# Keeping the residual stream in DRAM between the stages of a two-layer decoder, and eight more seven-product groups

## The chip, the cores and the metric

The kernel runs on one core of a Trainium2 chip. The metric is the device time of one execution in microseconds (us); a result is the median of several executions. The engines are named as in the profile: PE (TensorE, matrix products), DVE (VectorE), ACT (ScalarE), POOL (GpSimd), SP (SyncE, which here only issues transfers).

## The reference, cut to what matters

One sequence of 256 tokens of width 2048, in float32, goes through two layers:

```python
h = x
h = h + mamba2_mixer(rmsnorm(h, a_norm_w), a_in_proj, ..., a_out_proj)      # in-projection, scan, out-projection
h = h + (silu(g) * u) @ w_down[0]          # g, u = split(rmsnorm(h, f0) @ w_gate_up[0])
k, v, cum = shared_kv(h, kv_norm_w, w_kvf, b_f, k_norm_w)
h = h + forgetting_attention(rmsnorm(h, b_norm_w), k, v, cum, w_q, q_norm_w, w_o)
h = h + (silu(g) * u) @ w_down[1]          # g, u = split(rmsnorm(h, f1) @ w_gate_up[1])
```

Nearly all of the work is products of the 256 x K activations with large weights that are read once: in-projection (2048 x 10304), out-projection (4096 x 2048), gate/up (2048 x 11264, twice), down (5632 x 2048, twice), queries, keys and values (2048 x 2048 each), attention output (2048 x 2048).

## The kernel before

**Products.** A weight block is 512 rows by 512 columns; its K rows are four slices of 128. Each float32 weight is split into two parts, `hi` (ACT casts it, L272) and `lo` (DVE subtracts, L278), and each product of a slice with 128 tokens is three matmuls of 512 columns: activation hi by `whi`, activation hi by `wlo`, activation lo by `whi`. A *unit* is 512 KB of weights (two slices), loaded by SP into one of six buffers `wraw` (`RAW = 6`), split into one of four pairs of buffers `whi`/`wlo` (`SPL = 4`); a *piece* is what one split feeds, 12 matmuls. `stream` walks the pieces in a fixed order; it issues the splits four pieces ahead of the matmuls, and a load as soon as the splits that free its buffer have been issued. Work on results (adding to the residual, transposes, gating) is woven in by `flow`, a small planner with its own estimates.

**Pairs and groups.** `pair` multiplies the same activations with two column blocks, left and right. For a K block (`kg`) that is not listed in `crossed`, that is 4 units and 48 matmuls. For one that is listed, a `Group` computes the 2 x 2 block product (two token halves by two column blocks) with seven products in place of eight: 7 pieces in the order f, d, c, a, e, g, b, of 6 matmuls each, 42 in all. A group needs five loads: three plain units and two sums of weights (`c`, `a`), which are made in DRAM ahead of time: `next_sum` has SP copy one block to a `wsum` tensor and POOL add another to it by an accumulating transfer. When it is called is set by `PACE`, pairs of (end, n): up to load number `end`, one call every n loads. DVE forms two more sums within a group (L428). The activations of a listed block need their own sums, `xS` (a slot of the pool `slots`), made in `to_slot` where the block is written, or later by `add_sums`, half a block at a time: four sums on DVE, a cast on ACT, a subtraction on DVE.

**Which blocks are listed.** `WOUT` for the out-projection, `DN0` and `DN1` for the down projections, `(2,)` for the attention output, and in `ffn_up` `(1, 2)` for the gate/up pairs 1 to 9 and `(2,)` for the first and the last. If the last two listed numbers are neighbours, `pair` puts the second group behind the next plain left block.

**Residual.** `h` (256 x 2048, 16 KB of each partition) is a constant tile, loaded from `x` at load number 24 (`load_h`). At the end of each pair of the out, down and attention-output stages, `parts_to_h` and `done` add the results to it; `take` then transposes it into the slots of the next stage. There are 15 slots of 8 KB.

**Order of the stages.** In-projection with the scan (called "in" below), out-projection ("out"), gate/up ("gu0"), down ("dn0"), queries/keys/values with attention ("qkv"), attention output ("wo"), gate/up ("gu1"), down ("dn1").

Of the kernel before, what the change touches and what calls it, by code (L numbers as in the profile page):

```python
# [35 lines left out]

WOUT, DN0, DN1 = (4, 6), (3, 7), (3, 5, 7, 9)

# [3 lines left out]

PACE = ((24, 0), (224, 6), (440, 9), (760, 7), (2000, 9))

# [137 lines left out]
class Unit:  # L182


    def __init__(self, blk, kg, src, width, ks, step=2):
        self.blk, self.kg, self.src, self.width, self.ks = blk, kg, src, width, ks
        self.pieces = [list(range(a, min(a + step, len(ks)))) for a in range(0, len(ks), step)]
        self.raw, self.dead = None, False

# [42 lines left out]
def kernel(ctx: ExitStack, tc: tile.TileContext, xT_d, x_d, cols_d, rows_d, wdt_d, win_d,  # L232
# [4 lines left out]
    const = ctx.enter_context(tc.tile_pool(name="const", bufs=1))  # L237
    slots = ctx.enter_context(tc.tile_pool(name="slots", bufs=15))
    wraw = ctx.enter_context(tc.tile_pool(name="wraw", bufs=RAW))
# [67 lines left out]

    h = const.tile([P, NT, DM], F32, name="h")

# [26 lines left out]

    def pair(xs, sources, done, fills, crossed, parts):


        both = [Block(xs, d, f) for d, f in zip(done, fills)]  # L340
        x = Cross(*both, parts)
        order, rights = [], []
        adjacent = len(crossed) > 1 and crossed[-1] == crossed[-2] + 1
        for kg in range(len(xs)):
            us = [halves(b, kg, src[kg], ([0, 2], [1, 3])) for b, src in zip(both, sources)]
            if kg in crossed:
                if not (adjacent and kg == crossed[-1]):
                    order += rights
                    rights = []
                (b11, b21), (b12, b22) = us  # L350
                c, a = Sum(b22.src, b12.src), Sum(b22.src, b21.src)
                sums.extend((c, a))
                first = {"f": b12, "d": b21, "c": Unit(None, kg, c, NB, [1, 3]),
                         "a": Unit(None, kg, a, NB, [1, 3]), "g": b11}
                order.append(Group(x, first, xs[kg], kg == crossed[0], kg == crossed[-1]))
            else:
                for b, u in zip(both, us):
                    b.units += u
                order += us[0]
                rights += us[1]  # L360
        if adjacent:
# [120 lines left out]
    def stream(pre_load, pre_split):  # L482
# [12 lines left out]
        def load_on():  # L495
            while dead[0] < len(units) and units[dead[0]].dead:
                dead[0] += 1
            while loaded[0] < min(dead[0] + RAW, len(units)):
# [143 lines left out]
    def h_slot(dst, j, wcol):  # L642
        yield from to_slot(dst, lambda t, f: h[:, t, (4 * j + f) * P:(4 * j + f + 1) * P],
                           None if wcol is None else wcol + 4 * j)
# [25 lines left out]
    def of_h(j):  # L670
        return [[h[:, t, i * NB:(i + 1) * NB] for t in range(NT)] for i in (j, j + 1)]

# [21 lines left out]
    def out_stage(xs, w_d, wcol, crossed, summed=()):  # L694
# [5 lines left out]
        def done(j):  # L700
            def run(ps):
                for t in range(NT):
                    hb = h[:, t, j * NB:(j + 1) * NB]
                    yield tt(hb, hb, ps[t])
# [4 lines left out]
        def take(j):  # L709
            yield SYNC  # L710
            yield from h_slot(nxt[j], j, wcol)
            for t in range(NT):
                sumsq(h[:, t, j * NB:(j + 1) * NB], ss[:, t, j:j + 1])
                yield A(0.6)
# [5 lines left out]
        for j in (0, 2):  # L720
            pair(xs, w_d[j:j + 2], (done(j), done(j + 1)), nxt[j:j + 2], crossed, parts_to_h(j))
        return nxt, r

    def ffn_up(xs, r, gu_d, summed):
# [41 lines left out]
        for nb in range(NFB):  # L766
            x = [None]

            def took(y, x=x):
# [3 lines left out]
            pair(xs, gu_d[2 * nb:2 * nb + 2], (lambda ps, x=x: gate(x[0], ps), lambda ps, x=x, nb=nb: up(x[0], ps, nb)),  # L773
                 (None, acts[nb]), (1, 2) if 0 < nb < NFB - 1 else (2,), took)
        return acts
# [53 lines left out]
    def late_loads():  # L829
        nc.sync.dma_start(out=rows, in_=rows_d.partition_broadcast(P))  # L830

    x_v = x_d.rearrange("(t p) d -> p t d", p=P)

# [440 lines left out]
    def final(j):  # L1274
        def run(ps):
            cs = slice(j * NB, (j + 1) * NB)
            for t in range(NT):
                nc.vector.tensor_tensor(out=h[:, t, cs], in0=h[:, t, cs], in1=ps[t], op=ALU.add)
                nc.sync.dma_start(out=out_v[:, t, cs], in_=h[:, t, cs])
                yield V(0.6)  # L1280
        return run

    for j in (0, 2):
        pair(act1, dn1_d[j:j + 2], (final(j), final(j + 1)), (None, None), DN1, parts_to_h(j))

    pre_load = {2 * i: (lambda i=i: load_x(i)) for i in range(4)}
    pre_load[10] = late_loads
    pre_load[24] = load_h
    pre_split = {0: lambda: flow.advance(split_x(0)), 1: lambda: flow.advance(xs1[0].task),
# [91 lines left out]
```

## Time and profile before

| what | value |
|---|---|
| median of 3 runs | 2487.56 us (2487.37 to 2489.85) |
| the profiled execution | 2488.84 us, span from first to last instruction 2487.1 us |
| PE busy | 2475.1 us, 11422 matmuls |
| DVE busy | 1972.9 us |
| ACT busy | 1435.4 us |
| moved by transfers | 633.34 MB, mean 255 GB/s |

The profiled execution lies 1.74 us above its span and 1.28 us above the median of the runs. Matmuls are pipelined: one of 512 columns is listed with about 390 ns, but the next starts after about 227 ns. So durations of single matmuls are not added up; starts are compared.

### The profile page before, as it was taken

The page shows a single profiled execution, that of the slowest core. Times are in us where ns is not written, and L with a number is a line of the kernel's source. Part 1 is how long each engine was busy: PE and PEld are TensorE (multiplying, and loading weights), DVE is VectorE, ACT ScalarE, POOL GpSimd, SP SyncE. Part 2 cuts the span into 40 slices and gives each one's busy share as a digit, 9 for nine tenths or more (in the row PEclk, how much of TensorE's full clock was granted, in tenths as well). Part 3 has the DMA queues.
Part 4 walks back from the last instruction along what each step waited for, and adds up shares of the span by engine and source line. Part 5 has one row for each costly group of instructions (what it writes and reads, how often), then busy time and mean ns, then how long its engine had stood idle before and what let it go on. Part 6 is the DMA issues. An engine that isn't in the chain of part 4 may idle for free.

```text
span 2487.1 us, 31833 instructions
## 1 busy us (share of the span) xinstructions
PE 2475.1 (100%) x11422; PEld 2053.5 (83%) x11422; DVE 1972.9 (79%) x2555; ACT 1435.4 (58%) x1807; POOL 133.9 (5%) x168
## 2 busy tenths in 40 slices
PE   9999999999999999999999999999999999999999
PEld 7888888888888888888888888888888888888787
DVE  6677777778688999997766657678889999988867
ACT  6665566555555656564545556565565656555544
POOL 0000000000000000000000111010000000000000
PEclk9999999999999999999999999999999999999999
DMA  7877868778887888887888888677889898878765
GB/s 251 262 249 232 252 217 245 228 236 275 276 259 257 294 259 294 260 291 252 262 272 255 261 239 249 208 221 209 261 257 302 279 304 270 289 247 261 243 227 182
DMA packets 173167, 633.34 MB, mean 255 GB/s; under 512 B 19248, under 2 KB 19904, under 8 KB 171472
## 3 DMA queue, kind: packets, MB, share of 16 engines
q1 hardware_dynamic: 154800, 559.90, 64.3%
q0 software_dynamic: 18208, 71.39, 15.6%
q8 instruction: 90, 1.47, 0.2%
q14 instruction: 69, 0.57, 0.1%
HBM read 629.04 MB, written 123.81 MB: 303 GB/s over the span
## 4 chain that ended last, share of the span: by engine, by line
PE 97%; DVE 1%; DMA 1%; ACT 0%; issue 0%; SPq 0%; ACTq 0%; DVEq 0%
PE acc L554 23%; PE acc L556 23%; PE acc L555 23%; PE mis L469 4%; PE mis L466 4%; PE mis L467 4%; PE acc L467 3%; PE acc L469 3%; PE acc L466 3%; PE mis L586 1%; PE mis L1023 1%; DVE wlo L278 1%; PE mis L893 0%; DVE wraw L428 0%; DMA wraw<-in_dn_dram 0%; PE mis L1029 0%
## 5 line engine op out<-in xcount | busy, mean ns | idle before, releaser
L278 DVE TENSOR_TENSOR wlo<-wraw,whi 128x1024 fp32r<-128x1024 f32 (+1 forms) x959 | 1147.3, 1220 | 306.4 <-ACT whi L272 299.1
L272 ACT CAST whi<-wraw 128x1024 fp32r<-128x1024 f32 (+1 forms) x962 | 988.9, 1049 | 671.0 <-PE acc L556 457.1
L554 PE MATMUL acc<-whi,xT 128*128 128x512 f32 x2496 | 981.8, 393 | 2.3 <-ACT whi L272 2.2
L555 PE MATMUL acc<-wlo,xT 128*128 128x512 f32 x2496 | 972.6, 390 | 1.0 <-DVE wlo L278 1.0
L556 PE MATMUL acc<-whi,xT 128*128 128x512 f32 x2496 | 973.0, 390 | 0.0
L554 PEld LDWEIGHTS acc<-whi,xT 128*128 128x128 f32 x2496 | 469.2, 188 | 99.8 <-ACT whi L272 2.9
L556 PEld LDWEIGHTS acc<-whi,xT 128*128 128x128 f32 x2496 | 468.8, 188 | 98.4
L555 PEld LDWEIGHTS acc<-wlo,xT 128*128 128x128 f32 x2496 | 469.4, 188 | 97.4 <-DVE wlo L278 2.4
L280 DVE SCALAR_TENSOR_TENSOR wlo<-wraw,cols,whi 128x512 fp32r<-128x512 f32 x192 | 134.7, 747 | 72.0 <-ACT whi L274 71.5
L274 ACT ACTIVATE whi<-wraw,cols 128x512 fp32r<-128x512 f32 x192 | 127.6, 717 | 72.1 <-PE acc L556 55.1
L428 DVE TENSOR_TENSOR wraw<-wraw,wraw 128x1024 f32<-128x1024 f32 x116 | 142.1, 1225 | 4.0
L467 PE MATMUL mis<-wlo,xS 128*128 128x512 f32 x348 | 135.5, 389 | 0.4 <-DVE wlo L278 0.4
L469 PE MATMUL mis<-whi,xS 128*128 128x512 f32 x348 | 135.4, 389 | 0.0
L466 PE MATMUL mis<-whi,xS 128*128 128x512 f32 x348 | 135.4, 389 | 0.0
L377 POOL DMA_DIRECT2D wsum<-in_gu_dram x80 | 66.5, 831 | 1024.3 <-DMA wsum<-in_gu_dram 1004.7
L467 PE MATMUL acc<-wlo,xT 128*128 128x512 f32 x224 | 87.6, 391 | 1.8 <-DVE wlo L278 1.8
L469 PE MATMUL acc<-whi,xT 128*128 128x512 f32 x224 | 87.2, 389 | 0.0
L466 PE MATMUL acc<-whi,xT 128*128 128x512 f32 x224 | 87.2, 389 | 0.0
L467 PEld LDWEIGHTS mis<-wlo,xS 128*128 128x128 f32 x348 | 65.3, 188 | 14.6 <-DVE wlo L278 0.9
L466 PEld LDWEIGHTS mis<-whi,xS 128*128 128x128 f32 x348 | 65.3, 188 | 13.6
L469 PEld LDWEIGHTS mis<-whi,xS 128*128 128x128 f32 x348 | 65.3, 188 | 13.5
L272 ACT CAST xT<-mis 128x512 fp32r<-128x512 f32 x52 | 28.0, 589 | 54.5 <-PE mis L586 54.5
(250 smaller groups left out, 2104.0 us busy)
## 6 DMA issues: line engine op xcount, KB each, us to landing
wraw<-in_gu_dram SPq DMA_DIRECT2D x312, 512.0 KB, 6.3
wraw<-in_dn_dram SPq DMA_DIRECT2D x164, 512.0 KB, 5.8
wraw<-in_win_dram SPq DMA_DIRECT2D x159, 512.0 KB, 5.7
wraw<-wsum SPq DMA_DIRECT2D x116, 512.0 KB, 5.9
wsum<-in_gu_dram SPq DMA_DIRECT2D x80, 512.0 KB, 6.9
wsum<-in_gu_dram POOLq DMA_DIRECT2D x80, 512.0 KB, 8.6
wraw<-in_wout_dram SPq DMA_DIRECT2D x60, 512.0 KB, 6.2
wraw<-in_wq_dram SPq DMA_DIRECT2D x32, 512.0 KB, 5.4
```

The lines of the kernel that those rows point to most:

```text
L272: nc.scalar.copy(out=hi, in_=src)
L274: nc.scalar.activation(hi, src, AF.Copy, scale=scal)
L278: nc.vector.tensor_tensor(out=lo, in0=src, in1=hi.bitcast(F32), op=ALU.subtract)
L280: nc.vector.scalar_tensor_tensor(out=lo, in0=src, scalar=scal, in1=hi.bitcast(F32), op0=ALU.mult, op1=ALU.subtract)
L377: nc.gpsimd.dma_start(out=old.tile, in_=old.other, accum_op=ALU.add)
L428: nc.vector.tensor_tensor(out=us[out].raw, in0=us[in0].raw, in1=us[in1].raw, op=ALU.add)
L466: nc.tensor.matmul(ps, lhsT=xh, rhs=hi[:, p, :], start=group.first and p == 0 and name not in own, stop=False)
L467: nc.tensor.matmul(ps, lhsT=xh, rhs=lo[:, p, :], start=False, stop=False)
L469: nc.tensor.matmul(ps, lhsT=xl, rhs=hi[:, p, :], start=False, stop=stop and p == 1)
L554: nc.tensor.matmul(b.ps[t], lhsT=xh, rhs=hi[:, j, :], start=u is b.units[0] and ks[j] == 0, stop=False)
L555: nc.tensor.matmul(b.ps[t], lhsT=xh, rhs=lo[:, j, :], start=False, stop=False)
L556: nc.tensor.matmul(b.ps[t], lhsT=xl, rhs=hi[:, j, :], start=False, stop=last and j == len(ks) - 1)
```

## The change

`h` is no longer a constant. Each half of it (1024 columns, one slot of 8 KB) is fetched from DRAM into a slot while a pair is under way (`fetch_h`, two transfers on SP of 512 KB each), added to, written back by one transfer on ACT (`store_h`), and read by the next such stage. The two slots' worth of memory go to the pool (17 slots in place of 15). Eight more groups are listed: one more in each of the two pairs of out, dn0 and dn1, and one more in the last gate/up pair of each layer. Their numbers are moved, and `PACE` is set anew.

```diff
-WOUT, DN0, DN1 = (4, 6), (3, 7), (3, 5, 7, 9)
+WOUT, DN0, DN1 = (3, 5, 6), (3, 6, 9), (2, 4, 6, 8, 9)
...
-PACE = ((24, 0), (224, 6), (440, 9), (760, 7), (2000, 9))
+PACE = ((24, 0), (226, 6), (426, 8), (540, 6), (651, 5), (2000, 8))
...
-    slots = ctx.enter_context(tc.tile_pool(name="slots", bufs=15))
+    slots = ctx.enter_context(tc.tile_pool(name="slots", bufs=17))
...
-    h = const.tile([P, NT, DM], F32, name="h")
+
+    hs = [None, None]
+    h_d = [x_d.rearrange("(t p) d -> p t d", p=P)[:, :, i * 2 * NB:(i + 1) * 2 * NB] for i in range(2)]
+
+    def h_block(t, j):
+        return hs[j // 2][:, t, (j % 2) * NB:(j % 2 + 1) * NB]
+
+    def fetch_h(half):
+        hs[half] = slot([P, NT, 2 * NB], F32, "h")
+        for t in range(NT):
+            nc.sync.dma_start(out=hs[half][:, t], in_=h_d[half][:, t])
+
+    def store_h(half):
+        h_d[half] = dram.tile([P, NT, 2 * NB], F32, name=nm("h_d"))
+        nc.scalar.dma_start(out=h_d[half], in_=hs[half])
...
+                if kg == max(i for i in range(crossed[-1]) if i not in crossed):
+                    us[0][0].ahead = ahead
...
+                if units[i].ahead is not None:
+                    units[i].ahead()
                 load(units[i], i == 0, load_x0 if i < 2 else None)
...
         def take(j):
             yield SYNC
+            if j % 2:
+                store_h(j // 2)
             yield from h_slot(nxt[j], j, wcol)
...
         for j in (0, 2):
-            pair(xs, w_d[j:j + 2], (done(j), done(j + 1)), nxt[j:j + 2], crossed, parts_to_h(j))
+            pair(xs, w_d[j:j + 2], (done(j), done(j + 1)), nxt[j:j + 2], crossed, parts_to_h(j),
+                 lambda j=j: fetch_h(j // 2))
...
-                 (None, acts[nb]), (1, 2) if 0 < nb < NFB - 1 else (2,), took)
+                 (None, acts[nb]), (1, 2) if nb > 0 else (2,), took)
...
-    def load_h():
-        for t in range(NT):
-            nc.sync.dma_start(out=h[:, t], in_=x_v[:, t])
```

The order of the instructions shows three places of it.

SP, in the first pair of out: the last rows before the loads of the plain block that stands between the group at 3 and the group at 5 (`wraw` are weight buffers, `wsum` the sums in DRAM). Now:

```order
L392 DMA wsum_4563<-in_gu_dram 128x1024
L414 DMA wraw_4566<-in_wout_dram 128x1024
L414 DMA wraw_4593<-in_wout_dram 128x1024
L414 DMA wraw_4611<-wsum_680 128x1024
L414 DMA wraw_4652<-wsum_832 128x1024
L414 DMA wraw_4672<-in_wout_dram 128x1024
L318 DMA h_4701<-in_x_dram 128x1024 x2
L414 DMA wraw_4704<-in_wout_dram 128x1024
```

The residual's half is now asked for in the middle of the weights; before, all of it was asked for once, among the loads of in:

```order
L397 DMA wraw_509<-in_win_dram 128x1024
L397 DMA wraw_531<-in_win_dram 128x1024
L1075 DMA h<-in_x_dram 128x2048 x2
L397 DMA wraw_552<-in_win_dram 128x1024
L397 DMA wraw_575<-in_win_dram 128x1024
```

PE, at the first group of gu0 (its block of activations is number 2, its first product reads `xS`; `mis<-ident,h` are transposes of the residual for block 3). Before, the transposes of block 3 stood ahead of the group:

```order
L555 MATMUL acc_6049<-wlo_6040,xT_5269 128x512
L556 MATMUL acc_6049<-whi_6039,xT_5269 128x512
L466 MATMUL acc_6048<-whi_6064,xS_5978 128x512
L467 MATMUL acc_6048<-wlo_6065,xS_5978 128x512
L469 MATMUL acc_6048<-whi_6064,xS_5978 128x512
L466 MATMUL acc_6048<-whi_6064,xS_5978 128x512
L467 MATMUL acc_6048<-wlo_6065,xS_5978 128x512
L469 MATMUL acc_6048<-whi_6064,xS_5978 128x512
L466 MATMUL mis_6165<-whi_6096,xT_5947 128x512
```

and now they stand between its first and its second piece:

```order
L575 MATMUL acc_6069<-whi_6062,xT_5334 128x512
L483 MATMUL acc_6068<-whi_6084,xS_6056 128x512
L484 MATMUL acc_6068<-wlo_6085,xS_6056 128x512
L486 MATMUL acc_6068<-whi_6084,xS_6056 128x512
L483 MATMUL acc_6068<-whi_6084,xS_6056 128x512
L484 MATMUL acc_6068<-wlo_6085,xS_6056 128x512
L486 MATMUL acc_6068<-whi_6084,xS_6056 128x512
L605 MATMUL mis_6178<-ident,h_5473 128x128 x4
L605 MATMUL mis_6187<-ident,h_5473 128x128 x4
L483 MATMUL mis_6206<-whi_6119,xT_6025 128x512
```

So what ACT and DVE do for block 3 falls into the group, and the group is reached sooner after block 2's transposes.

DVE, ahead of the first group of dn1. Before (group at 3), the last write of its `xS_3865` is followed by two splits for earlier pieces, then comes the first split of the group, `wlo_3887`:

```order
L278 TENSOR_TENSOR wlo_3874_19326<-wraw_3848_19182,whi_3873_19325 128x1024
L278 TENSOR_TENSOR xS_3865_19276<-ysum_3872_19319,xS_3865_19276 128x4x128
L278 TENSOR_TENSOR wlo_3879_19348<-wraw_3854_19208,whi_3878_19347 128x1024
L637 TENSOR_TENSOR ysum_3881_19365<-xT_3474_17500 128x512
L615 TENSOR_TENSOR ysum_3881_19365<-ysum_3881_19365 128x128
```

Now (group at 2), the last write of its `xS_3936` stands behind the first two splits of the group itself, `wlo_3944` and `wlo_3948`:

```order
L278 TENSOR_TENSOR wlo_3944_19461<-wraw_3917_19319,whi_3943_19460 128x1024
L656 TENSOR_TENSOR ysum_3946_19478<-xT_3299_16576 128x512
L278 TENSOR_TENSOR wlo_3948_19481<-wraw_3920_19339,whi_3947_19480 128x1024
L634 TENSOR_TENSOR ysum_3946_19478<-ysum_3946_19478 128x128
L635 TENSOR_TENSOR ysum_3946_19478<-ysum_3946_19478 128x128
L636 TENSOR_TENSOR ysum_3946_19478<-ysum_3946_19478 128x128
L637 TENSOR_TENSOR ysum_3946_19478<-ysum_3946_19478 128x128
L278 TENSOR_TENSOR xS_3936_19430<-ysum_3946_19478,xS_3936_19430 128x4x128
L278 TENSOR_TENSOR wlo_3950_19503<-wraw_3925_19361,whi_3949_19502 128x1024
```

The sums have moved up to the products that need them; the `xS` of the second group (at 4) stands as close. Over the whole program PE has 48 matmuls less; SP has 38 transfers more (16 copies for sums, 8 loads of weights, and 16 of 512 KB for the residual in place of 2 of 1 MB), POOL 16 accumulating transfers more, ACT 6 transfers for the residual.

## Rows read from the trace of the kernel before

**Rows 1.** The page, busy time and share of the span of each engine:

```profile
PE 2475.1 (100%) x11422; PEld 2053.5 (83%) x11422; DVE 1972.9 (79%) x2555; ACT 1435.4 (58%) x1807; POOL 133.9 (5%) x168
```

**Rows 2.** The page, the chain that ended last, by engine:

```profile
PE 97%; DVE 1%; DMA 1%; ACT 0%; issue 0%; SPq 0%; ACTq 0%; DVEq 0%
```

**Rows 3.** Waits of PE: total us, times, longest us:

```profile
PE acc L554 <- ACT whi L272: 2.2, 2, 1.6
PE acc L467 <- DVE wlo L278: 1.8, 3, 0.6
...
PE mis L586 <- DVE h L674: 1.0, 2, 0.8
...
PE mis L467 <- DVE wlo L278: 0.4, 1, 0.4
```

**Rows 4.** Timeline of PE in out: start us, listed us, first and last matmul:

```profile
568.65 0.39 PE L466 MATMUL acc<-whi,xS 128*128 128x512 f32 x1
...
577.94 0.39 PE L469 MATMUL acc<-whi,xT 128*128 128x512 f32 x1
578.17 0.39 PE L554 MATMUL acc<-whi,xT 128*128 128x512 f32 x1
...
589.05 0.39 PE L466 MATMUL acc<-whi,xS 128*128 128x512 f32 x1
```

**Rows 5.** Groups by line and shape, DVE: count, busy us, mean ns, idle before:

```profile
L278 DVE TENSOR_TENSOR wlo<-wraw,whi 128x1024 fp32r<-128x1024 f32 x957 | 1146.0, 1221 | 304.8 <-ACT whi L272 297.6
```

**Rows 6.** Timeline of DVE in dn1, in a group: start us, us:

```profile
2304.16 0.68 DVE L278 TENSOR_TENSOR xS<-ysum,xS 128x512 fp32r<-128x512 f32 x1
2304.88 0.69 DVE L637 TENSOR_TENSOR ysum<-xT 128x512 f32<-128x512 f32 x1
...
2306.55 1.22 DVE L278 TENSOR_TENSOR wlo<-wraw,whi 128x1024 fp32r<-128x1024 f32 x1
2307.80 1.22 DVE L428 TENSOR_TENSOR wraw<-wraw,wraw 128x1024 f32<-128x1024 f32 x1
2308.94 2.50 DVE L278 TENSOR_TENSOR wlo<-wraw,whi 128x1024 fp32r<-128x1024 f32 x2
```

**Rows 7.** Windows of three groups, in out, gu0 and dn1:

```profile
core 0: us, PE busy (x) PEld busy (x) DVE busy (x) ACT busy (x) POOL busy (x), PEclk, DMA share, GB/s
588.54:598.14 9.60, 9.60 (x43) 7.80 (x43) 9.41 (x9) 6.35 (x8) 0.81 (x1) 1.00 0.85 261
719.82:730.30 10.48, 9.91 (x43) 7.81 (x43) 9.65 (x10) 7.11 (x9) 1.53 (x2) 1.00 0.70 163
2304.80:2316.16 11.36, 10.31 (x44) 7.83 (x44) 11.08 (x15) 6.40 (x7) 0.82 (x1) 1.00 0.71 186
```

**Rows 8.** Waits of ACT in out (540 to 720 us), for transfers:

```profile
ACT whi L272 <- DMA wraw<-in_wout_dram: 4.3, 1, 4.3
```

**Rows 9.** The chain in order of time, from 716 and from 2284 us:

```profile
718.60 1.22 ACT junk L577 x4
...
2291.25 7.74 DMA wraw<-in_dn_dram
```

**Rows 10.** The page, DMA queues: packets, MB, share of 16 engines over the span:

```profile
q1 hardware_dynamic: 154800, 559.90, 64.3%
q0 software_dynamic: 18208, 71.39, 15.6%
```

**Rows 11.** Windows of the stages out, dn0, wo and gu1, columns as in Rows 7:

```profile
521.71:695.78 174.07, 173.96 (x785) 143.53 (x785) 134.94 (x165) 100.52 (x131) 11.09 (x13) 1.00 0.85 267
...
1159.40:1396.89 237.49, 237.49 (x1065) 197.07 (x1065) 161.06 (x171) 116.53 (x130) 10.59 (x13) 1.00 0.84 261
...
1693.96:1787.13 93.17, 92.13 (x433) 76.60 (x433) 77.91 (x113) 56.98 (x89) 4.10 (x5) 1.00 0.76 237
1787.13:2250.64 463.51, 462.89 (x2089) 383.57 (x2089) 412.99 (x426) 277.93 (x312) 21.12 (x26) 1.00 0.87 279
```

**Rows 12.** Window of the busiest transfers in gu1, columns as in Rows 7:

```profile
1980.00:2010.00 30.00, 30.00 (x134) 24.86 (x133) 26.88 (x29) 16.98 (x18) 1.66 (x2) 1.00 0.97 311
```

More of the change, by code (lines that the diff above doesn't have):

```diff
@@ L187, in __init__ @@
         self.pieces = [list(range(a, min(a + step, len(ks)))) for a in range(0, len(ks), step)]
-        self.raw, self.dead = None, False
+        self.raw, self.dead, self.ahead = None, False, None
 class Sum:
@@ L335, in narrow, with pair @@
         blocks.append(b)
-    def pair(xs, sources, done, fills, crossed, parts):
+    def pair(xs, sources, done, fills, crossed, parts, ahead=None):
         both = [Block(xs, d, f) for d, f in zip(done, fills)]
@@ L642, in h_slot @@
     def h_slot(dst, j, wcol):
-        yield from to_slot(dst, lambda t, f: h[:, t, (4 * j + f) * P:(4 * j + f + 1) * P],
+        yield from to_slot(dst, lambda t, f: h_block(t, j)[:, f * P:(f + 1) * P],
                            None if wcol is None else wcol + 4 * j)
@@ L670, in of_h @@
     def of_h(j):
-        return [[h[:, t, i * NB:(i + 1) * NB] for t in range(NT)] for i in (j, j + 1)]
+        return [[h_block(t, i) for t in range(NT)] for i in (j, j + 1)]
     def tt(out, in0, in1, op=ALU.add):
@@ L702, in run @@
                 for t in range(NT):
-                    hb = h[:, t, j * NB:(j + 1) * NB]
+                    hb = h_block(t, j)
                     yield tt(hb, hb, ps[t])
@@ L710, in take @@
             yield SYNC
+            if j % 2:
+                store_h(j // 2)
             yield from h_slot(nxt[j], j, wcol)
             for t in range(NT):
-                sumsq(h[:, t, j * NB:(j + 1) * NB], ss[:, t, j:j + 1])
+                sumsq(h_block(t, j), ss[:, t, j:j + 1])
                 yield A(0.6)
@@ L830, in late_loads @@
         nc.sync.dma_start(out=rows, in_=rows_d.partition_broadcast(P))
-    x_v = x_d.rearrange("(t p) d -> p t d", p=P)
     def dt_done(psT):
@@ L1275, in run @@
         def run(ps):
-            cs = slice(j * NB, (j + 1) * NB)
             for t in range(NT):
-                nc.vector.tensor_tensor(out=h[:, t, cs], in0=h[:, t, cs], in1=ps[t], op=ALU.add)
-                nc.sync.dma_start(out=out_v[:, t, cs], in_=h[:, t, cs])
+                hb = h_block(t, j)
+                nc.vector.tensor_tensor(out=hb, in0=hb, in1=ps[t], op=ALU.add)
+                nc.sync.dma_start(out=out_v[:, t, j * NB:(j + 1) * NB], in_=hb)
                 yield V(0.6)
@@ L1283 @@
     for j in (0, 2):
-        pair(act1, dn1_d[j:j + 2], (final(j), final(j + 1)), (None, None), DN1, parts_to_h(j))
+        pair(act1, dn1_d[j:j + 2], (final(j), final(j + 1)), (None, None), DN1, parts_to_h(j),
+             lambda j=j: fetch_h(j // 2))
     pre_load = {2 * i: (lambda i=i: load_x(i)) for i in range(4)}
     pre_load[10] = late_loads
-    pre_load[24] = load_h
     pre_split = {0: lambda: flow.advance(split_x(0)), 1: lambda: flow.advance(xs1[0].task),
```

## The prediction

> **What bounds the kernel now.** I read the page's busy times first: PE is busy for 2475.1 of 2487.1 us [rows 1]. As a busy PE need not be a PE at its peak, I then read the chain that ended last: 97% of it is PE, 1% DVE, 1% transfers [rows 2]. So PE is waited for, hardly ever made to wait. The waits of PE say how much there is to win besides: six kinds, 2.2 us for the largest and 0.4 for the last, 7.8 us in all [rows 3]. Any real gain must therefore come from fewer matmuls, and the question is whether DVE, ACT and the transfers still keep up.
>
> **What a group saves.** In out, a group's first matmul starts at 568.65 and the next plain one at 578.17: 42 matmuls in 9.52 us, 0.227 us each. The plain blocks that follow run to 589.05: 48 in 10.88 us [rows 4]. A group saves 1.36 us. There are eight more: 8 x 1.36 = 10.9 us off PE. Nothing hides these; they lie on the chain. Further gain could only come from waits that happen to vanish at the places that move; of the 7.8 us I allow 1 us for that [rows 3].
>
> **What the eight groups cost DVE and ACT.** A plain block needs four splits, a group seven, and two additions on DVE. The split is listed with 1.22 us, but in a full queue the next instruction starts 1.14 us later (2307.80 to 2308.94) [rows 5, 6]. So DVE needs 9 x 1.14 = 10.3 us in a group where PE needs 9.5, and 4.6 in a plain block where PE needs 10.9. A group eats about 0.7 us of lead, more with the hand-offs between ACT and DVE; one plain block gives back some 6, up to the four buffers' limit. New `xS` come with it: half of one takes from 2304.16 to 2306.55, 2.4 us [rows 6], 4.8 for a block, for one more block in out, dn0 and dn1. In the middle gate/up pairs, which have two groups already, PE is busy 462.89 of 463.51 us [rows 11], so the two last gate/up pairs, which become like them, I cost at nothing. Elsewhere the place decides. I go through it by the nearest groups [rows 7].
>
> Start of dn1: the first group moves from block 3 to block 2, so there are 22 instead of 33 us of PE time (two or three plain blocks) to finish the last gate/up result and the first `xS`; and there are five `xS` in place of four to form during the stage. From the first to the fourth group (4 x 9.5 + 3 x 10.9 = 70.7 us of PE) DVE has 4 x 10.3 + 3 x 4.6 = 55 us of weights plus four `xS`, 4 x 4.8 = 19: 74, more than PE has. (With only the bare starts of an `xS`, 4.1 us, it is 71.) Before, with only two `xS` left to form in the same stretch, it was 55 + 2 x 4.8 = 65. So a lead that is lost is not won back. The nearest row is the group at 2304.80, which took 11.36 us for its 9.52: 1.84 lost [rows 7], behind a load that took 7.74 us [rows 9]. Bounds: 0, and three more groups that lose as much, 5.5. I take 2.5, since the lead at the stage's start covers the first group or two.
>
> Start of gu0: the group at 719.82 took 10.48 us, 0.96 lost [rows 7], and the chain runs there through ACT, which squares the residual for the norm in front of the splits (1.22 us) [rows 9]. In the new order ACT's and DVE's work on block 3 falls into this group as well: four casts and four subtractions of some 0.4 us each. Bounds: 0, and 2.5 for the 1.6 us on ACT and as much of hand-offs as today; I take 1.0, as part of it lies beside PE.
>
> Groups of out: the first moves from block 4 to 3 while DVE still forms `xS`. The group at 588.54 lost only 0.08 (9.60 for 9.52), though DVE was busy 9.41 of 9.60 us [rows 7] and a load had come 4.3 us late for ACT in this stage [rows 8]. So the four buffers swallow a lateness of about that size, and have little left for more.
>
> **What the transfers cost.** The shares of the queues give the price [rows 10]: plain transfers 0.643 x 2487.1 / 559.90 = 2.86 us of all 16 engines per MB, POOL's 0.156 x 2487.1 / 71.39 = 5.43. A load of 512 KB is 1.50 us; a sum (copy and accumulation) 1.50 + 2.85 = 4.35; a half of the residual 3.0, in or out. As a check, out before: 68 loads and 11 sums, 149.9 us of 174.07, a share of 0.86; the window says 0.85 [rows 11]. After, by the order of SP's transfers: out 70 loads, 11 sums, two fetches and one store, 161.9 us of 171.4, 0.945; dn0 94 loads, 16 sums, 219.6 of 234.8, 0.935; wo 34 loads, 6 sums, 86.1 of 93.2, 0.92; gu1 197 loads, 25 sums, 407.3 of 462.2, 0.88. Before, these stood at 0.85, 0.84, 0.76 and 0.87 [rows 11]. A window of 30 us ran at 0.97 with PE busy 30.00 [rows 12]. So on the mean all of it fits. What remains are bunches: a fetch puts 3.0 us ahead of the weights on SP, and a store's 3.0 us goes beside them. For out, where the slack was used up already, bounds 0 and 3.0 (the whole fetch), taken 1.0. For all other stages, and the end of the program, bounds 0 and 3.0, taken 0.5. SP's new wait for a slot I cost at nothing: by the order, the fetches in the middle of the program wait for readers hundreds of instructions earlier; if that cover were gone, the loads behind them on SP would be late. The stores' issue on ACT stands behind additions already done; the same holds.
>
> The page "HBM Reference" of the Trainium skill (Specifications) gives about 358 GB/s as the effective bandwidth of a core, its share when both cores of a pair stream. By that, reads and writes of out (63 MB), dn0 (86 MB) and wo (33.5 MB) would take 176, 240 and 94 us, some 10 us more than PE needs, and the sum would come to about zero. The trace does not agree: in the busiest window 311 GB/s were moved, and with what two sums write besides, 2.1 MB in 30 us, that is about 380 GB/s without a wait of PE [rows 12]. The sum goes by the rows.
>
> **The sum.** -10.9 + 2.5 (dn1) + 1.0 (gu0) + 1.0 (out) + 0.5 (rest) = -5.9 us. Against the profiled execution (2488.84, 1.74 beyond its span of 2487.1) that is 2482.9; it lies 1.28 above the median of the runs, 2487.56, to which my number refers: 2481.7. With all costs at their lower bounds and 1 us of waits gone it is 2475.7; with all at their upper bounds (5.5 + 2.5 + 3.0 + 3.0 = 14.0) 2490.7.
>
> **Rivals.**
> 1. All is hidden: the buffers swallow the new lateness everywhere, cost at most 2.5 us. For it: the window at 0.97 [rows 12], and the groups in gate/up. Against it: the two groups that lose time today [rows 7]. Time 2476.5 to 2479.
> 2. The waits eat the gain: dn1 and gu0 near their upper bounds and out near its, -10.9 + 5.5 + 2.5 + 2.5 = -0.4; time about 2487. For it: DVE's 74 us against PE's 71 in dn1. Against it: a group at today's density loses nothing when it starts with a full lead.
> 3. Slower, by the transfers alone: in out, dn0 and wo they become the bound. If the 16 engines carry in the long run only 0.90 of what the price above says, the three stages take 467.6 / 0.90 = 519.6 us where PE needs 499.4: 20 us lost, net +9, time 2497. It decides below a share of 0.91, where the loss passes the gain by 5 us. For it: no whole stage today runs above 0.87 [rows 11], and loads already come late at times [rows 8, 9]. Against it: the window at 0.97 [rows 12].
>
> **How the numbers follow.** Forecast (net -4 to -8.5): 0.42, its own range 2479 to 2483.5. Rival 1: 0.22; rival 2 (net -4 to +5): 0.26; rival 3: 0.10. A measurement of this kernel tells changes of over 0.2%, 5.0 us, from none. Rival 1 and about seven in ten of the forecast's cases are faster by more than that: 0.52; the rest of the forecast and rival 2 are within it: 0.38; slower 0.10. The range, 2476 to 2489.5, leaves out rival 3 and the worst of rival 2.
>
> **What would show it.** Right: PE with 48 matmuls less; PE's waits risen from 7.8 by a few us, most for `wlo` in the first 90 us of dn1 and in the first group of gu0; groups there that take 10 to 11.5 us; shares of 0.92 to 0.95 in out and dn0 with PE busy. Rival 1: no wait there. Rival 2: several groups of dn1 at 11 us or more. Rival 3: ACT waiting for `wraw` transfers in out, dn0 and wo for tens of us, and these stages no shorter than now. I would be wrong altogether if SP stood at a fetch for a slot or for a store's landing, with all weights queued behind it.

## The result, and the profile after

The changed kernel takes 2515.26 us, median of 4 runs (2513.23 to 2516.24); the kernel before takes 2488.55 us beside it. The ratio is 1.0105, with a 95% interval of 1.0092 to 1.0117: slower by some 27 us, where 6 us of gain were forecast. The profiled execution took 2515.99 us, its span is 2514.2.

The page of the changed kernel, busy times and the chain by engine:

```profile
PE 2476.7 (99%) x11374; PEld 2048.1 (81%) x11374; DVE 2031.2 (81%) x2631; ACT 1460.6 (58%) x1837; POOL 148.1 (6%) x184
...
PE 90%; DVE 5%; DMA 2%; ACT 1%; issue 1%; SPq 0%; DVEq 0%; ACTq 0%
```

PE has its 48 matmuls less, and is busy longer than before all the same [rows 1]. On the chain DVE's share has risen from 1% to 5% [rows 2]: some 126 of 2514 us now run through DVE. The transfers' share is 2%. So the first look already speaks against the transfers. The waits of PE say where (total us, times, longest us):

```profile
PE acc L573 <- DVE h L693: 11.3, 3, 5.8
PE acc L573 <- DVE h L1294: 5.5, 1, 5.5
PE acc L484 <- DVE wlo L278: 3.7, 6, 0.7
PE mis L484 <- DVE wlo L278: 3.5, 5, 0.8
PE mis L483 <- DVE xT L280: 2.0, 1, 2.0
```

The first two rows have no forerunner in [rows 3]. L573 is the first product of a plain block; L693 and L1294 are the additions of results to the residual `h`. A matmul into an accumulator waits for an addition that *reads* an accumulator. The pool `acc` has four banks, two for the left and two for the right column block; the next pair's first product must write the left banks, and DVE has not read them out yet.

The stages out, gu0, dn0, wo, gu1 and dn1, as windows (columns as in [rows 7]):

```profile
522.44:712.03 189.59, 175.20 (x773) 142.29 (x772) 154.38 (x190) 107.44 (x139) 11.10 (x13) 0.97 0.87 274
712.03:1177.83 465.80, 463.49 (x2082) 383.88 (x2083) 415.37 (x427) 279.89 (x313) 21.95 (x26) 1.00 0.87 276
1177.83:1412.45 234.62, 234.40 (x1046) 193.71 (x1044) 174.52 (x190) 120.59 (x132) 12.22 (x15) 1.00 0.92 296
1711.19:1804.41 93.22, 92.18 (x434) 76.46 (x432) 77.95 (x112) 56.97 (x89) 4.90 (x6) 1.00 0.88 277
1804.41:2267.06 462.65, 461.78 (x2083) 382.59 (x2083) 417.29 (x429) 281.41 (x315) 20.27 (x25) 1.00 0.88 281
2267.06:2514.20 247.14, 232.71 (x1005) 188.73 (x1003) 202.30 (x228) 124.61 (x129) 6.54 (x8) 0.98 0.76 247
```

Against [rows 11], dn0 is 2.87 us shorter at a DMA share of 0.92, and each of its six groups takes 9.52 us, so its two new groups save their 2.7 there. Not all of the 2.87 is gain, though: 24 transposes of `h` lay in this window before and 16 do now; the other eight, 0.8 us, have moved behind its end, into qkv. The transposes `mis<-ident,sq` of qkv stand behind them (before, then changed; the last times are their first and last start):

```profile
L1131 PE MATMUL mis<-ident,sq x64: 270/272/277, 1431.2 to 1662.4; 128*128 128x128 f32 x64
...
L1147 PE MATMUL mis<-ident,sq x64: 270/272/277, 1447.7 to 1678.9; 128*128 128x128 f32 x64
```

From the start of dn0 to the first of them it was 271.8 us (from 1159.4) and is 269.9 (from 1177.83): 1.9 us gained. wo is where it was at a share of 0.88 instead of 0.76, and gu1 gained 0.9 of 1.4. The loss stands in two stages: out is 15.5 us longer with two groups more (189.59 for 174.07), and dn1 some 11 us (its window before ran from 2250.64 to the end of the span at 2487.1). In both the mean granted clock is below 1.

The end of out's first pair shows how. PE (start us, listed us), the last plain block and the next pair's first products:

```profile
613.34 0.39 PE L575 MATMUL acc<-whi,xT 128*128 128x512 f32 x1
619.01 0.76 PE L573 MATMUL acc<-whi,xT 128*128 128x512 f32 x1 [5.27 <-DVE h L693]
619.57 0.63 PE L574 MATMUL acc<-wlo,xT 128*128 128x512 f32 x1
...
623.41 0.47 PE L574 MATMUL acc<-wlo,xT 128*128 128x512 f32 x1
623.71 0.39 PE L575 MATMUL acc<-whi,xT 128*128 128x512 f32 x1
```

and DVE meanwhile:

```profile
607.26 0.69 DVE L693 TENSOR_TENSOR h<-h,d 128x512 f32<-128x512 f32 x1
...
611.65 0.68 DVE L693 TENSOR_TENSOR d<-mis,d 128x512 f32<-128x512 f32 x1
612.25 1.21 DVE L278 TENSOR_TENSOR wlo<-wraw,whi 128x1024 fp32r<-128x1024 f32 x1
613.39 0.68 DVE L693 TENSOR_TENSOR h<-h,w 128x512 f32<-128x512 f32 x1
...
617.05 1.22 DVE L278 TENSOR_TENSOR wlo<-wraw,whi 128x1024 fp32r<-128x1024 f32 x1
618.18 1.88 DVE L693 TENSOR_TENSOR h<-h,acc 128x512 f32<-128x512 f32 x3
```

From 607.26 on DVE works off the eight additions that the group's other results need (`parts_to_h`), with splits between them; only at 618.18 comes the first `h<-h,acc`, which frees a left bank, and PE starts again at 619.01. Had PE gone on, the first product would have stood at 613.57: 5.4 us lost. Then ten matmuls follow one another at 0.43 us instead of 0.227 (619.57 to 623.41 is nine of them, 3.84 us), another 2 us: the granted clock from 619.01 to 623.71 is 0.52, near the lower of the two levels (1.2 GHz), behind a stand of 5.4 us; PE had been busy at the upper one (2.4 GHz) until then. The page "TensorE: Matmul & The Clock Gate" of the Trainium skill (Part 1, "Wait — 56ns, not 53.3ns?") gives 426.7 ns from start to start for 512 columns at the lower level; the trace agrees. One such place costs some 7.6 us. There are three: between the pairs of out, at its end (5.81 us of idle time in front of gu0's first product), and between the pairs of dn1 (5.50). At out's end and in dn1 it is the same picture, with eight and 13 matmuls at 0.43 us. Together, counted in the same way, that is some 24 us (the expectations below say 23).

What made them is an order that the part ahead of the prediction tells in one sentence and the prediction does not price. The new lists end in neighbours, `WOUT` in 5, 6 and `DN1` in 8, 9; `pair` then puts the last group behind the last plain left block. The last group's product e releases the eight additions. Before, PE went from e to the next pair over two pieces of the group and four plain ones, 2 x 1.36 + 4 x 2.72 = 13.6 us; now over two and two, 8.2 us. For DVE nothing has changed: the two additions that free the left banks stood behind the eight others before as well, and at the end of out's first pair it takes 10.92 us in both kernels from the first of the eight to the first `h<-h,acc`. In the kernel before that was just in time. DVE there, before:

```profile
598.30 0.68 DVE L674 TENSOR_TENSOR h<-h,d 128x512 f32<-128x512 f32 x1
...
609.22 1.27 DVE L674 TENSOR_TENSOR h<-h,acc 128x512 f32<-128x512 f32 x2
```

and PE, its last plain product and the next pair's first:

```profile
609.55 0.39 PE L556 MATMUL acc<-whi,xT 128*128 128x512 f32 x1
610.05 0.47 PE L554 MATMUL acc<-whi,xT 128*128 128x512 f32 x1
```

PE's first product starts 0.83 us after the first reading of a left bank starts, as it does now (618.18 to 619.01), and 0.27 us behind its own pace. At the other two places the distance before was 0.83 us too, without any delay. So there was no lead to use up: 5.4 us less of PE's work between e and the next pair became 5.4 us of waiting.

The rest of the loss is groups with late splits. The first two groups of out, the first of gu0, and the first three of dn1:

```profile
557.81:570.29 12.48, 10.45 (x43) 7.65 (x42) 11.32 (x14) 7.47 (x8) 0.83 (x1) 1.00 0.81 247
581.46:592.87 11.41, 10.13 (x43) 7.73 (x42) 11.17 (x14) 6.75 (x8) 0.00 (x0) 1.00 0.84 243
736.58:749.28 12.70, 10.68 (x52) 8.63 (x50) 12.46 (x17) 11.47 (x21) 3.19 (x3) 1.00 0.72 255
2289.72:2300.47 10.75, 10.10 (x43) 7.73 (x42) 10.31 (x10) 6.60 (x7) 0.00 (x0) 1.00 0.72 196
2311.61:2323.05 11.44, 10.17 (x44) 7.72 (x42) 11.19 (x14) 6.78 (x8) 0.00 (x0) 1.00 0.77 209
2334.25:2345.71 11.46, 10.14 (x44) 7.73 (x42) 11.30 (x15) 6.52 (x7) 0.00 (x0) 1.00 0.88 277
```

Over 9.52 us these are 3.0 and 1.9 in out and 1.2, 1.9 and 1.9 in dn1, with about 0.3 more each in the plain pieces behind a group. In gu0 eight transposes (0.8 us) have come into the window; the rest of the 3.2 us over 9.52, 2.4, is lost, where 1.0 was lost before. Some 5.4 in out, 6 in dn1 and 2.4 in gu0 make near 14 us. About 3 of them were lost before as well: 1.0 in gu0, and some 2 at the group of dn1 in [rows 7] and behind it. The balance: -10.9 + 24 + 11 = 24, for a span that grew by 27.1. The other 3 us lie spread over several stages (0.7 in the stage in, 0.8 in dn0 with the start of qkv, 0.5 in gu1) and are not put down to a cause.

### The profile page after: what moved, and what is told of

Its sections match the earlier page's. It is cut to its first block, busy times and chain, and to the rows that moved or that the text cites. A ratio compares the mean times of both kernels' runs of the same rounds, so it can differ in the third digit from the quotient of the medians.

```text
span 2514.2 us, 31997 instructions
## 1 busy us (share of the span) xinstructions
PE 2476.7 (99%) x11374; PEld 2048.1 (81%) x11374; DVE 2031.2 (81%) x2631; ACT 1460.6 (58%) x1837; POOL 148.1 (6%) x184
## 4 chain that ended last, share of the span: by engine, by line
PE 90%; DVE 5%; DMA 2%; ACT 1%; issue 1%; SPq 0%; DVEq 0%; ACTq 0%
PE acc L573 21%; PE acc L574 21%; PE acc L575 21%; PE mis L483 4%; PE mis L486 4%; PE mis L484 4%; PE acc L484 3%; PE acc L486 3%; PE acc L483 3%; DVE wlo L278 3%; PE mis L605 1%; ACT whi L272 1%; PE mis L1043 1%; DVE wraw L445 1%; DMA wraw<-in_gu_dram 1%
## 5 line engine op out<-in xcount | busy, mean ns | idle before, releaser
L278 DVE TENSOR_TENSOR wlo<-wraw,whi 128x1024 fp32r<-128x1024 f32 (+1 forms) x983 | 1174.6, 1219 | 282.9 <-ACT whi L272 272.8
L272 ACT CAST whi<-wraw 128x1024 fp32r<-128x1024 f32 (+1 forms) x986 | 1011.4, 1049 | 662.1 <-PE acc L575 403.7
L573 PE MATMUL acc<-whi,xT 128*128 128x512 f32 x2368 | 935.2, 395 | 18.8 <-DVE h L693 11.3
L574 PE MATMUL acc<-wlo,xT 128*128 128x512 f32 x2368 | 926.1, 391 | 1.2 <-DVE wlo L278 1.2
L575 PE MATMUL acc<-whi,xT 128*128 128x512 f32 x2368 | 925.5, 391 | 0.0
L573 PEld LDWEIGHTS acc<-whi,xT 128*128 128x128 f32 x2368 | 446.8, 189 | 114.1 <-issue 19.9
L574 PEld LDWEIGHTS acc<-wlo,xT 128*128 128x128 f32 x2368 | 447.0, 189 | 94.6 <-DVE wlo L278 4.2
L575 PEld LDWEIGHTS acc<-whi,xT 128*128 128x128 f32 x2368 | 446.5, 189 | 93.9
L445 DVE TENSOR_TENSOR wraw<-wraw,wraw 128x1024 f32<-128x1024 f32 x132 | 161.7, 1225 | 4.5
L484 PE MATMUL mis<-wlo,xS 128*128 128x512 f32 x396 | 154.8, 391 | 3.5 <-DVE wlo L278 3.5
L483 PE MATMUL mis<-whi,xS 128*128 128x512 f32 x396 | 154.2, 389 | 2.0 <-DVE xT L280 2.0
L486 PE MATMUL mis<-whi,xS 128*128 128x512 f32 x396 | 154.1, 389 | 0.0
L484 PE MATMUL acc<-wlo,xT 128*128 128x512 f32 x256 | 100.4, 392 | 3.7 <-DVE wlo L278 3.7
L486 PE MATMUL acc<-whi,xT 128*128 128x512 f32 x256 | 99.7, 390 | 0.0
L483 PE MATMUL acc<-whi,xT 128*128 128x512 f32 x256 | 99.7, 389 | 0.0
L484 PEld LDWEIGHTS mis<-wlo,xS 128*128 128x128 f32 x396 | 74.3, 188 | 21.4 <-DVE wlo L278 6.0
L483 PEld LDWEIGHTS mis<-whi,xS 128*128 128x128 f32 x396 | 74.3, 188 | 17.9 <-ACT junk L596 2.4
L486 PEld LDWEIGHTS mis<-whi,xS 128*128 128x128 f32 x396 | 74.4, 188 | 15.2
L484 PEld LDWEIGHTS acc<-wlo,xT 128*128 128x128 f32 x256 | 48.0, 188 | 16.4 <-DVE wlo L278 6.5
```

Source lines behind the costliest of these rows:

```text
L272: nc.scalar.copy(out=hi, in_=src)
L278: nc.vector.tensor_tensor(out=lo, in0=src, in1=hi.bitcast(F32), op=ALU.subtract)
L445: nc.vector.tensor_tensor(out=us[out].raw, in0=us[in0].raw, in1=us[in1].raw, op=ALU.add)
L483: nc.tensor.matmul(ps, lhsT=xh, rhs=hi[:, p, :], start=group.first and p == 0 and name not in own, stop=False)
L484: nc.tensor.matmul(ps, lhsT=xh, rhs=lo[:, p, :], start=False, stop=False)
L486: nc.tensor.matmul(ps, lhsT=xl, rhs=hi[:, p, :], start=False, stop=stop and p == 1)
```

## The experiments

The theory, called W in the expectations: neighbours at the end of a list make PE wait for accumulator banks (23 us), and besides, groups that come while DVE forms `xS` are late (14 us). Rival T: the residual's fetches, stores and slots cost the time. Rival D: a group costs DVE as much as it saves PE, wherever it stands.

| run | median us | ratio to before, 95% interval |
|---|---|---|
| residual in DRAM alone | 2487.51 | 1.0000, 0.9990 to 1.0009 |
| neighbours alone | 2513.59 | 1.0105, 1.0089 to 1.0120 |
| groups not interleaved | 2494.0 | 1.0023, 1.0013 to 1.0034 |
| left banks read out first | 2495.4 | 1.0029, 1.0018 to 1.0040 |
| four added groups | 2484.42 | 0.9987, 0.9978 to 0.9996 |
| more groups in second pairs | 2492.3 | 1.0014, 1.0005 to 1.0023 |
| `xS` additions on POOL | 2521.25 | 1.0132, 1.0118 to 1.0146 |
| `xS` additions left out | 2485.63 | 0.9989, 0.9980 to 0.9998 |
| `xS` of second pairs formed late | 2501.76 | 1.0053, 1.0039 to 1.0067 |

**The residual in DRAM alone.** The changed kernel with the lists and `PACE` of before:

```diff
-WOUT, DN0, DN1 = (3, 5, 6), (3, 6, 9), (2, 4, 6, 8, 9)
+WOUT, DN0, DN1 = (4, 6), (3, 7), (3, 5, 7, 9)
-PACE = ((24, 0), (226, 6), (426, 8), (540, 6), (651, 5), (2000, 8))
+PACE = ((24, 0), (224, 6), (440, 9), (760, 7), (2000, 9))
-                 (None, acts[nb]), (1, 2) if nb > 0 else (2,), took)
+                 (None, acts[nb]), (1, 2) if 0 < nb < NFB - 1 else (2,), took)
```

> The residual in DRAM with its fetches, stores and 17 slots, but the old lists, the old PACE and so the old number of groups. Theory W (a wait for accumulator banks, made by neighbours at the end of a list): no neighbours in out and dn1, so no PE wait for the adds of the residual above 1 us, and 2488.5 us within 3. Rival T (fetches, stores and slots of the residual cost the time): most of the loss stays, 2505 or more, with PE or ACT waiting for h or wraw. Rival D (DVE has too much to do with the added groups): 2488.5 as in W.

2487.51 us, ratio 1.0000. The fetches and stores, 17 slots and all the code around them cost nothing that can be measured. T is out, and so is the prediction's rival 3 as far as the residual goes.

**Neighbours alone.** The kernel before, nothing else changed, and as many groups as it had:

```diff
-WOUT, DN0, DN1 = (4, 6), (3, 7), (3, 5, 7, 9)
+WOUT, DN0, DN1 = (5, 6), (3, 7), (3, 5, 8, 9)
```

> The kernel before, the residual a constant tile, as many groups as before; only WOUT (4,6) becomes (5,6) and DN1 (3,5,7,9) becomes (3,5,8,9). Theory W: three waits of 5 to 6 us of PE's first product of a pair for the adds to h, each with about 2 us of matmuls at half speed behind it: 3 x 7.7 = 23 us, 2508 to 2513. Rivals T and D: nothing that they blame has been added; 2488.5 within 3.

2513.59 us, at the upper end of W's range: 25 us slower, nearly all that the whole change lost. PE's waits, the first three (L674 and L1278 are this kernel's additions to `h`):

```profile
PE acc L554 <- DVE h L674: 10.6, 2, 5.3
PE acc L554 <- DVE h L1278: 5.3, 1, 5.3
PE mis L466 <- DVE xT L280: 2.3, 1, 2.3
```

Three waits at the three places, without one added group and without the residual in DRAM. Neither T nor D can explain it. This is the run that names the cause. The third row stands in the first group of gu0, and the changed kernel has it too (2.0 us, its row with `xT`). Here as there, eight transposes of `h` have fallen into this group; where out's list does not end in neighbours, as in the run with four added groups, they stand ahead of it and there is no such row. So gu0's late group comes with the neighbours in out as well. It loses 1.6 us more than before, and with that W's 23 us come near the 25 measured.

**Two ways to take the waits away.** First, the changed kernel with the last two groups one behind the other, the plain blocks after them:

```diff
-        adjacent = len(crossed) > 1 and crossed[-1] == crossed[-2] + 1
+        adjacent = crossed == (1, 2)
```

> The changed kernel, but in out and dn1 the two last listed groups stand one right behind the other, and the plain left and right blocks follow them. Same products, transfers and slots. Theory W: the three waits for banks go (-23 us), and two groups in a row cost DVE 20.6 us where PE needs 19, some 2 to 3 us at each of four places: 2493 to 2504. Rival T: 2515 as before it. Rival D: denser groups, so 2515 or more.

Second, the changed kernel with PE's order as it is, but DVE reads the left banks before it makes the eight additions (`rest` is what `parts_to_h` returned; the lines that hand it in are left out here. For such a group it is no longer started at product e, and in dn1 the store of these columns follows behind it):

```diff
                 for t in range(NT):
                     hb = h_block(t, j)
                     yield tt(hb, hb, ps[t])
                 yield EVAC
+                if rest is not None:
+                    yield from rest()
...
```

> The changed kernel with the same order on PE; where a group closes the left block, DVE first adds the left accumulators to h and only then makes the eight additions of the group's other results (in the last stage the store of these columns follows behind them). Theory W: the banks come free some 5 to 6 us sooner, the three waits go or fall under 1 us: 2515 - 23 = 2492, 2489 to 2497. Rivals T and D: DVE has as much to do and the transfers are the same: 2512 to 2518.

2494.0 and 2495.4 us, both in the range. In the second PE runs on across the end of out's first pair; DVE there (us):

```profile
602.04 5.91 DVE L278 TENSOR_TENSOR wlo<-wraw,whi 128x1024 fp32r<-128x1024 f32 x5
607.86 1.28 DVE L694 TENSOR_TENSOR h<-h,acc 128x512 f32<-128x512 f32 x2
```

The banks are free at 609.1, where the pair ends at 611.9. With the same matmuls, splits and transfers, 20 us came back by the order of ten additions. It is 4 us short of 24, for the lateness partly moved: gu0's first group took 16.18 us where it took 12.70 in the changed kernel, and PE's waits now hold two that were not there, both in this group,

```profile
PE acc L486 <- DVE xS L278: 2.1, 1, 2.1
PE acc L483 <- ACT xS L272: 1.7, 1, 1.7
```

since the left block's `xS` for the next stage now begins only behind the eight additions.

**Why groups are late.** The groups at the start of out and dn1 are as late as before in that second kernel: out's first took 12.49 us (556.12 to 568.61) against 12.48. On this kernel the additions that `add_sums` makes for `xS` were once moved to POOL (here the first of five; the other four go by the last argument) and once left out, the `xS` being split straight from the activations, so that this kernel's results are not the reference's and only its time counts. The `xS` of the gate/up stages, which `to_slot` makes, are as before in both. To POOL:

```diff
-                nc.vector.tensor_tensor(out=y, in0=part[0], in1=part[1], op=ALU.add)
-                yield V(0.66)
-                yield from sums_from(dst, half, y, x)
+                nc.gpsimd.tensor_tensor(out=y, in0=part[0], in1=part[1], op=ALU.add)
+                yield Q(0.9)
+                yield from sums_from(dst, half, y, x, nc.gpsimd)
...
```

> The kernel with DVE's early additions to h, and the additions that form the xS of out, dn0, dn1 and the attention output (one of 128x512 and four of 128x128 per half) moved from DVE to POOL; only the subtraction of the split stays on DVE. That takes some 1.7 us per half off DVE. If DVE's xS work makes the first groups late (5.4 us in out, 6.1 in dn1): these waits fall below 2 us in all, 2495.4 - 10 = 2485, 2483 to 2488, unless POOL itself is late with the sums. If the density of the groups alone does: 2494 to 2497.

Left out (against the same lines):

```diff
+                if half == 0:
+                    dst.sums = slot([P, 4, 2, 2, P], F32R, "xS")
+                split(dst.sums[:, :, 0, half, :], dst.sums[:, :, 1, half, :], part[0].rearrange("p f (a t) -> p (f a) t", t=P))
+                yield A(0.6) + V(0.6)
```

> The same question without POOL: the kernel with DVE's early additions to h, but those xS are split straight from the activations; the additions that form them are left out, so the products of these groups are not the reference's. DVE's xS work makes the first groups late: 2483 to 2488. The density of the groups: 2494 to 2497. If this run gains and the one with POOL doesn't, POOL is late or slows DVE.

Left out: 2485.63 us, 9.8 less. In PE's waits no row for `wlo` at a group's products (L484) is left, where there were 7.1 us; the `xS` waits at gu0 stay. The first two groups of dn1, 10.75 and 11.44 us long in the changed kernel, are 9.52 us each (PE; start of the group, and of the plain product behind it):

```profile
2274.18 0.39 PE L483 MATMUL acc<-whi,xS 128*128 128x512 f32 x1
...
2283.70 0.39 PE L574 MATMUL acc<-whi,xT 128*128 128x512 f32 x1
...
2294.57 0.39 PE L483 MATMUL acc<-whi,xS 128*128 128x512 f32 x1
...
2304.09 0.39 PE L574 MATMUL acc<-whi,xT 128*128 128x512 f32 x1
```

So the density of the groups alone costs nothing here; DVE's additions for `xS` in front of them do. Some 2 of the 9.8 us are the lateness in dn1 that the kernel before had too. For gu0's first group, whose `xS` this edit leaves alone, the run shows nothing. But POOL is no place for it, 2521.25 us, a miss by 36 us. DVE in that kernel from 2290 to 2360 us, groups by line (count, busy us, mean ns, and the idle time before them):

```profile
L278 DVE TENSOR_TENSOR wlo<-wraw,whi 128x1024 fp32r<-128x1024 f32 x29 | 43.3, 1530 | 1.6 <-ACT whi L272 1.5
...
L278 DVE TENSOR_TENSOR xS<-ysum,xS 128x512 fp32r<-128x512 f32 x8 | 5.5, 689 | 12.6 <-ACT xS L272 12.6
```

and POOL in the same stretch:

```profile
L657 POOL TENSOR_TENSOR ysum<-xT 128x512 f32<-128x512 f32 x7 | 10.8, 1542 | 18.3 <-DVE xS L278 18.3
L635 POOL TENSOR_TENSOR ysum<-ysum 128x128 f32<-128x128 f32 x8 | 10.1, 1267 | 0.5
```

Two things go wrong. DVE stood idle for 12.6 us in front of the split of `xS`, waiting for ACT and behind it POOL, and the groups' splits that came next in its queue did not start. And a split of weights took 1.53 us on the mean in place of 1.22: the twelve of the 29 that ran clear of POOL's additions still took 1.21 to 1.23, while seven that ran beside them took 2.17 to 2.32. The page "SBUF — State Buffer" of the Trainium skill (SBUF: two separate sides) says that GpSimd and a DVE operation with two inputs from SBUF take a pair of ports by turns, each for its whole instruction; the trace agrees: the split that began at 2308.62, while an addition of POOL ran, took 2.19 us.

**Only the groups that cost nothing.** The changed kernel with the old lists in out and dn1:

```diff
-WOUT, DN0, DN1 = (3, 5, 6), (3, 6, 9), (2, 4, 6, 8, 9)
+WOUT, DN0, DN1 = (4, 6), (3, 6, 9), (3, 5, 7, 9)
```

> The changed kernel with the old lists in out (4,6) and dn1 (3,5,7,9), so four added groups are left: one in each pair of dn0, one in the last pair of each gate/up stage. Theory W with its second part (the added groups of out and dn1 come while DVE forms xS): nothing that loses time is left, and four groups give 4 x 1.36 = 5.4 us: 2488.3 - 5.4 = 2482.9, 2481 to 2485. Rival D (added groups cost DVE as much as they save PE, wherever they stand): 2487 to 2490.

2484.42 us, ratio 0.9987 (0.9978 to 0.9996): 3.5 us faster than the kernel before, where 5.4 were expected. It lies within W's range and outside D's, which starts 0.1 us above the upper end of the interval. The windows of out, gu0, dn0 and gu1:

```profile
521.60:695.06 173.46, 173.46 (x785) 143.57 (x784) 135.89 (x166) 100.00 (x130) 11.07 (x13) 1.00 0.88 283
695.06:1157.83 462.77, 461.88 (x2083) 382.46 (x2083) 417.85 (x429) 279.94 (x314) 20.30 (x25) 1.00 0.88 281
1157.83:1392.46 234.63, 234.40 (x1045) 193.74 (x1044) 174.58 (x190) 120.61 (x132) 13.04 (x16) 1.00 0.91 295
1784.64:2246.72 462.08, 461.45 (x2084) 382.61 (x2083) 417.32 (x429) 279.58 (x313) 21.12 (x26) 1.00 0.88 282
```

gu1 gains its group in full (1.4 us against [rows 11]). dn0's window is 2.9 us shorter, but the same eight transposes are out of it; up to the transposes of qkv 1.9 of 2.7 are gained. gu0, which lay between 695.78 and 1159.40 before (463.62 us), gains 0.8 of 1.4.

**More groups in the second pairs only**, where the `xS` already exist. As the run before, with (2, 4, 6) in out's second pair and (1, 3, 5, 7, 9) in dn1's:

```diff
...
-    xs2, r2 = out_stage(ys, wout_d, C_F0, WOUT, summed=(1, 2))
+    xs2, r2 = out_stage(ys, wout_d, C_F0, ((4, 6), (2, 4, 6)), summed=(1, 2))
...
-        pair(act1, dn1_d[j:j + 2], (final(j), final(j + 1)), (None, None), DN1, parts_to_h(j),
+        pair(act1, dn1_d[j:j + 2], (final(j), final(j + 1)), (None, None), ((3, 5, 7, 9), (1, 3, 5, 7, 9))[j // 2], parts_to_h(j),
```

The lines left out make `out_stage` take a list for each pair, and `WOUT` and `DN1` name all blocks that need an `xS`.

> As the run with four added groups, and one more group in the second pair alone of out (2,4,6) and of dn1 (1,3,5,7,9); the first pairs keep (4,6) and (3,5,7,9). In the run with DVE's early additions the second pairs of out and dn1 lost nothing with three and five groups. If the xS formed in the first pair are what makes groups late: two more groups free of cost, 2.7 us less than the run with four groups, about 2480. If the number of groups in a pair is: 2483 to 2486, with PE waiting for wlo in the second pairs.

2492.3 us, not 2480; neither expectation held. The two `xS` that the second pairs need were still formed in the first pairs, and there `wlo` came late. Out is 1.1 us longer than in the run with four groups and dn1 1.0, though one more group should have made each 1.36 shorter: 2.5 and 2.4 us lost. The larger part stands elsewhere, 2.3 us in gu0 and 3.8 in wo. The window of wo:

```profile
1694.14:1791.35 97.21, 93.94 (x433) 77.58 (x432) 78.18 (x112) 57.53 (x90) 5.71 (x7) 0.98 0.85 267
```

against 93.43 us with four groups. There the chain holds a load of 9.95 us, with the splits and the additions to `h` late behind it: PE's transposes of `h` wait 2.4 us, and seven matmuls follow at 0.43 us (granted clock 0.50 from 1747.89 to 1751.00), another 1.5 us. Between 1700 and 1760 us the loads of wo took 9.9 us in the median instead of 7.5. As `PACE` counts loads, one load more ahead of wo moves the copies for sums against the residual's transfers; whether that is the cause was not tried.

**The same, with these `xS` formed after the first pair's additions:**

```diff
             yield tt(r1, r1, w)
+            for s in late if j == 0 else ():
+                add_sums(s)
...
```

> As the run with one more group in the second pair of out (2,4,6) and of dn1 (1,3,5,7,9), but the xS of these two groups is formed only once the first pair's additions to h are issued, not in the first pair. If forming it in the first pair is what cost 7.9 us there: no added wait for wlo in the first groups of out and dn1, 2484.4 - 2.7 = 2481.7 at best, up to 2484.5 if the new first group of a second pair is itself late, since DVE then has the additions to h and the xS to do in 11 to 22 us of PE. If the further groups (their loads, sums and splits) are what costs: 2489 or more, as before it.

2501.76 us, a miss. The waits for `wlo` that the last run had added in the first pairs went, and others came, at the second pairs' first groups, which took 15.3 us in out and 13.3 in dn1 (its profiled execution, at 2507.28, is its slowest):

```profile
PE acc L483 <- ACT xS L272: 4.3, 3, 1.7
PE acc L573 <- DVE h L1296: 2.9, 2, 2.2
...
PE acc L486 <- DVE xS L278: 2.4, 2, 1.8
```

At the start of a second pair DVE has the first pair's additions to `h` to make; the new `xS` stands behind them, and in dn1 it even delays the reading of the banks.

## Why the prediction was wrong, point by point

**The step that failed.** The part on out, dn1 and gu0 went through the groups "by the nearest groups" and priced splits, `xS` and hand-offs. It did not follow the order that neighbours at the end of a list make, though the part ahead of the prediction tells it in one sentence: which piece completes the left block, what stands ahead of the additions that free its banks, and who needs these banks. "So PE is waited for, hardly ever made to wait" hid that the pairs' ends had no slack. The waits of [rows 3] could not tell it, for a buffer that comes free just in time makes no wait; the starts at 609.22 and 610.05 in the kernel before tell it, and the prediction has no row of that place. The sum had no term for it, and no rival had it. Measured: three waits of 5.3 to 5.8 us, with about 2 us of lower clock behind each, 24 us; alone, in the kernel before, 25 us with gu0's late group.

**Terms that were mis-sized.** For late groups in out the sum had no term at all: "the four buffers swallow a lateness of about that size", and the 1.0 us for out, bounds 0 to 3.0, was the price of a fetch. They cost 5.4. The nearest row chosen, the group at 588.54, was one whose `xS` had been formed by 566 us; in the changed kernel DVE forms them until 592 us, and the two late groups lie at 558 to 593. In dn1 2.5 were taken, bounds 0 to 5.5. The late groups cost 6 there, some 4 more than before: within the bounds, but more than the value taken, which leaned on a lead that was gone within the first group (1.2 us lost). The mechanism told for dn1, DVE's `xS` among the splits, was right, as the run without these additions shows, and it holds for out as well. In gu0 1.0 was taken and 1.4 more than before measured. Block 3 did fall into the group, as foretold; that the neighbours in out put it there was not seen.

**What held.** A group saves 1.36 us: the six of dn0 take 9.52 us each, though of the stage's 2.7 us only 1.9 are left at qkv's transposes. The transfers were priced rightly and do not bound: dn0 ran at a share of 0.92 (0.935 foretold) with PE busy, and the residual in DRAM alone costs nothing. SP did not stand at a fetch: its wait for a slot came to 0.6 us in all. The two gate/up pairs cost little: gu1 gained 0.9 of its 1.4 us in the changed kernel and all of it in the run with four added groups, gu0 0.8 there. Rival 2 had the sign of its cause, waits that eat the gain, but was sized by late groups alone. Rival 3 had the right side and a cause that is not there, so that its direction came true was luck. The sentence that the trace does not agree with 358 GB/s goes too far: that figure is, by the prediction's own words, a core's share when both cores of a pair stream, and here one core is at work.

**What stays open.** The 1.9 us between 5.4 expected and 3.5 measured with four groups lie just within the interval; 0.8 of them stand in dn0 and the start of qkv and 0.6 in gu0, without a cause shown. The late loads in wo in the run with more groups in the second pairs were seen, not explained.

## What to carry to other kernels

When an edit changes which piece comes last before a boundary, follow the buffers, not the work: for each accumulator bank, name the instruction that frees it, what stands ahead of that one in its engine's queue, and who writes the bank next. An engine that is 97% of the chain with no wait above 1.6 us tells nothing of how near the next wait is; the slack at the boundaries has to be read too, as the distance from the release of a buffer to its next use. And add work to the stage where the engine that feeds has its lead; the same group took 9.5 us in dn0, and 12.5 and 11.4 at the start of out.

## What was not expected of the hardware

A wait of PE of 5 to 6 us cost about 2 us more than itself: ten, eight and 13 matmuls at 0.43 us in the three places, 1.8 to 2.8 us. The wait of 2.4 us in wo, directly behind eight transposes, cost 1.5 more; behind the one of 2.0 us in gu0, where full matmuls stood ahead, the granted clock stayed at 1.00 (743.74 to 747.00 us). And POOL's additions slowed DVE's splits from 1.22 to 1.53 us on the mean and were slowed themselves: the first of 128x128 took 1.27 us on the mean, where those clear of DVE's work took 0.46, and one of 128x512 took 1.54 on the mean, where DVE needs 0.69 [rows 6].
